# Value projection of seven head pairs: rounded and rest weights as one moving operand of 512 columns

## The chip, the cores and the metric

The kernel runs on one core of one Trainium2 chip. The metric is the device time of an execution in microseconds (us). A core has several engines that run side by side, each through a queue of its own: PE (matrix products), DVE, ACT and POOL (elementwise work), and SP, which here issues most transfers. "Row" below means one line of a view of the profile, or one instruction in an engine's order.

## The reference, cut to what matters

```python
def hybrid_mixer(h, lower_bound, w_in, ...):
    proj = h @ w_in
    xa, ga, q, f, v, g, m_a, m_b = jnp.split(proj, SPLIT_POINTS, axis=-1)
    ...
    vf = v.astype(jnp.float32).reshape(B_, S_, HG_HEADS, HG_DV)
    o = rms_norm(hgrn2_chunkwise(qf, kf, log_f, vf), hg_norm)
    ...
    return y @ w_out

def reference(x, ...):
    for l in range(DEPTH):
        h = rms_norm(x, norm_mix[l])
        x = x + hybrid_mixer(h, ...)
        h = rms_norm(x, norm_mlp[l])
        x = x + jnp.square(jax.nn.relu(h @ w_up[l])) @ w_down[l]
    return rms_norm(x, norm_final)
```

All is float32: 1024 rows of 1024 channels, 8 heads, an MLP of width 4096, one layer. The part in question is the slice v of `h @ w_in`: 1024 rows times 1024 channels of v, the sum over 1024 channels of h.

## The kernel before

Products in float32 are made from products of a shorter type. Each operand is split into a rounded part (suffix H) and a rest (suffix L), and the helper `mm3` (L157) adds three products into one PSUM bank: rounded times rounded, rounded times rest, rest times rounded. The rounded part is a cast on ACT (L94, L120), the rest a subtraction on DVE (L98); weights that are met a second time have their rest fetched back from DRAM by SP instead.

The mixer works on two halves of the rows (c = 0, 1; 512 rows each) and four pairs of heads (p = 0 to 3; 256 channels each): eight pairs of indices, one stage each. A stage projects, on PE, pj_xa, pj_q and pj_f (two banks of 128 channels by 512 rows each, weights standing still and rows moving), the gates of the recurrence pr and pi, and the values pv. The rest of the stage is the recurrence of one pair: DVE builds q, qa, qb, kb, kc, kk and qf by chains of products (L681 for all of them), PE makes small products of them (sc at L691, L811 and L822), PE turns kk around (pk, L848), multiplies it by v (pkv, L858), DVE carries the state (sn, L867 and L869), and PE makes the outputs po (L883, L886). POOL and ACT do smaller steps. Stages overlap: while PE projects for one pair, DVE works on the pair before.

The values are projected the other way round from the rest: 128 rows of h stand still (tile hT, parts H and L, 8 blocks k of 128 channels), and 256 columns of weights move. `v_steps` does this for seven of the eight pairs, for four row tiles tt of 128 rows, with 8 steps k of three matmuls each; one PSUM bank of 512 columns is taken for each row tile, and its first 256 columns are filled. ACT copies them to the tile v (L548). The pair (0,0) is projected in `first_norm` by other code. The callback `between` runs after a row tile: after the first it emits the end of the recurrence of the RG-LRU, after the second the transposes poT of outputs (L559).

The weights of the mixer come in tiles of 128 x 1024, each as two tiles with the tag "w" (rounded wH, rest wL) from one pool with six slots. The pool is also used by some weights of the gates and the MLP (names wA and ws). A slot that is to be filled again waits for the last reader of the tile that was in it. PSUM has banks under three tags: four "pj", two "sc", two "hg", handed round in turn.

The order on PE is pinned in the mixer (`pin`): it is the order of the code. The order on the other engines comes from a scheduler that goes by dependencies and priorities; `tc.high_priority(400)` moves an instruction ahead of its place. Where the MLP passes from its hidden rows to the down projection the order of PE is the scheduler's too.

Of the kernel before, what the change touches and what calls it, by code (L numbers as in the profile page):

```python
# [11 lines left out]
F32R = mybir.dt.float32r  # L12
U8 = mybir.dt.uint8
AF = mybir.ActivationFunctionType
ALU = mybir.AluOpType
# [3 lines left out]
P = 128  # L19
# [26 lines left out]
def trunk(ctx: ExitStack, tc: tile.TileContext, x, wts, mlp, pv, gains, mask_f, mask_u, out):  # L46
    nc = tc.nc
    V, A, G, PE = nc.vector, nc.scalar, nc.gpsimd, nc.tensor

    const = ctx.enter_context(tc.tile_pool(name="const", bufs=1))  # L50
    wp = ctx.enter_context(tc.tile_pool(name="wp", bufs=1))
# [55 lines left out]
    def load_w(i):  # L107
        raw = raw_tile(f"raw{i}")
        nc.sync.dma_start(raw, seq[i])
        return raw  # L110

    def split_w(i, raw):
        if i < n_mix + 3:
            h, lo = (wp.tile([P, 1024], F32R, tag="w", name=f"w{q}{i}", bufs=6) for q in "HL")
        else:
            h, lo = (kept[0].tile([P, 1024], F32R, tag=f"k{q}{i - n_mix}", name=f"w{q}{i}") for q in "HL")
        at = pair_tiles[i] if i < len(pair_tiles) else None
        with tc.high_priority(400):
            if at in rests:
                A.copy(h, raw)  # L120
                nc.sync.dma_start(lo.bitcast(F32), rests[at])
                return h, lo
            split(raw, h, lo)
        if at is not None and at in pair_tiles[i + 1 :]:
            rests[at] = dram.tile([P, 1024], F32, tag=f"rest{at}", name=f"rest{at}")
            nc.sync.dma_start(rests[at], lo.bitcast(F32))
        return h, lo
# [14 lines left out]
    used = [0]  # L142

    def next_w():
        used[0] += 1
        return get_w(used[0] - 1)
# [3 lines left out]
    def pin(ins):  # L150
        if pinned[0]:
            tc.keep_in_program_order(ins)

    def mm3(o, ah, al, bh, bl, first, last, goes_on=False, chain=None):
        how = {"skip_group_check": True} if goes_on else {}
        for a, b, begins, ends in ((ah, bh, first, False), (ah, bl, False, False), (al, bh, False, last)):
            ins = PE.matmul(o, a, b, start=begins, stop=ends, **how)  # L157
            pin(ins)
            if chain is not None:
                edge = mybir.DependencyInfo(mybir.DependencyClass.NoSync, mybir.DependencyReason.DATA)  # L160
                if chain:
                    tc.add_manual_dep(ins.ins, chain[-1].ins.name, edge, reason="last products")
                chain.append(ins)
# [142 lines left out]
    def first_norm():  # L306
# [73 lines left out]
        ws, pv = {}, {}  # L380

        def w_high(i):
            ws[i] = tuple(wp.tile([P, 1024], F32R, tag="w", name=f"w{q}{i}", bufs=6) for q in "HL")
            keep(A.copy(ws[i][0], xraws[i]))

        def w_low(i):
# [6 lines left out]
        v = mt("v", "v_00", (P, 4, 256))  # L393
# [139 lines left out]

    def v_steps(c, p, got, between):
        v = mt("v", f"v_{c}{p}", (P, 4, 256))
        w = [next_w(), next_w()]
        for tt in range(4):
            pp = bank("sc" if tt == 2 else "pj", f"pv_{c}{p}_{tt}")
            for k in range(8):
                hh, hl = kt(hT[c], k)  # L540
                cut = slice(tt * P, (tt + 1) * P)
                cols = slice((k % 4) * 256, (k % 4 + 1) * 256)
                wh, wl = w[k // 4]
                mm3(pp[:, :256], hh[:, cut], hl[:, cut], wh[:, cols], wl[:, cols], k == 0, k == 7)
                if k % 2:
                    if k < 7:
                        yield
            A.copy(v[:, tt, :], pp[:, :256])  # L548
            between(tt)
            yield  # L550
        got["v"] = v
# [540 lines left out]
    def quad_steps(i, pools, raws=raw_tile, minus=False):  # L1092

        ops = ops_w[i] = {}
        s = []

        def sums(behind=None):
            ra, rb = (r.rearrange("p (a b) -> p a b", a=2) for r in raw_q[i])
            a11, a21, a12, a22 = ra[:, 0, :], ra[:, 1, :], rb[:, 0, :], rb[:, 1, :]
            s.extend(raws(f"s{i}{h}") for h in range(2))  # L1100
            sa, sb = (r.rearrange("p (a b) -> p a b", a=2) for r in s)
            ins = V.tensor_tensor(out=sa[:, 0, :], in0=a21, in1=a22, op=ALU.add)  # L1102
            if behind is not None:
                how = mybir.DependencyInfo(mybir.DependencyClass.NoSync, mybir.DependencyReason.DATA)
                tc.add_manual_dep(ins.ins, behind.ins.name, how, reason="sums")
            if minus:
                V.scalar_tensor_tensor(sa[:, 1, :], sa[:, 0, :], -1.0, a11, op0=ALU.mult, op1=ALU.subtract)
            else:
                V.tensor_tensor(out=sa[:, 1, :], in0=sa[:, 0, :], in1=a11, op=ALU.add)
            V.tensor_tensor(out=sb[:, 0, :], in0=a21, in1=a11, op=ALU.add)  # L1110
            V.tensor_tensor(out=sb[:, 1, :], in0=a12 if minus else sa[:, 1, :], in1=sa[:, 1, :] if minus else a12, op=ALU.subtract if minus else ALU.add)

        def single(behind=None):
            t = pools[0].tile([P, 2, 512], F32R, tag="w1", name=f"wA11{i}", bufs=2)
            split(raw_q[i][0][:, 0:512], t[:, 0, :], t[:, 1, :], behind)
            ops["A11"] = (t[:, 0, :], t[:, 1, :])

        def pair(src, names):
            def go(pool=None, tag=None, bufs=None, lo_behind=None):
                if pool:  # L1120
                    t = pool.tile([P, 2, 1024], F32R, tag=tag, name=f"w{names[0]}{i}", bufs=bufs)
                    h, lo = t[:, 0], t[:, 1]
                else:
                    h, lo = (pools[1].tile([P, 1024], F32R, tag="w", name=f"w{names[0]}{i}{q}", bufs=6) for q in "HL")
                split(src(), h, lo, None, lo_behind, (names[0], i))
                for j, o in enumerate(names):
                    cols = slice(j * 512, (j + 1) * 512)
                    ops[o] = (h[:, cols], lo[:, cols])

            return go  # L1130

        return {
            "sums": sums,
            "a": single,
            "b": pair(lambda: s[0], ("s1", "s2")),
            "c": pair(lambda: s[1], ("s3", "s4")),
            "d": pair(lambda: raw_q[i][1], ("A12", "A22")),
        }
# [9 lines left out]
    for o in ("t1", "n2", "T4", "T3"):  # L1148
        pool = np_ if o in ("t1", "n2") else tp
# [314 lines left out]
    for part in range(2):  # L1464
# [4 lines left out]
        for hf in range(2):  # L1469
            pp = {tt: bank("pj", f"po1{hf}{tt}") for tt in tts}  # L1470
# [16 lines left out]
            for tt in tts:  # L1487
                cols = slice(hf * 512, (hf + 1) * 512)
# [271 lines left out]
    for kb in range(n_kb):  # L1760
        last = kb + 1 == n_kb
        qs = order[2 * kb : 2 * kb + 2]
        for half in range(2):
# [33 lines left out]
            for step, (bk, wo, uo), prs in [  # L1797
# [111 lines left out]
```

## Time and profile before

| | |
|---|---|
| time, three runs | 1534.24, 1535.8 and 1536.2 us, median 1535.8 |
| time of the profiled execution | 1535.65 us |
| its span | 1533.9 us, mean granted clock of PE 0.999 |
| HBM over the span | 199 GB/s, 201.50 MB read, 103.81 MB written |
| mixer stages with the edited code | from about 116 us to 545 us |

The span runs from the first to the last instruction in the record; the time has the 1.75 us around it as well. "Busy" counts an engine's own instructions, not its waits. Rows of a timeline give the start in us from the span's start, the length in us, the engine, the line, the operation, and output<-inputs by tile names without buffer numbers; at the end, in brackets, how long the engine was idle before and what ended that. In the rows of PE the lengths of successive matmuls overlap.

### The profile page before, as it was taken

How to read it: one execution, taken by the hardware profiler on the slowest of the kernel's cores; microseconds unless marked ns; L12 is line 12 of the kernel's file. 1: busy time of each engine (PE TensorE's matmuls, PEld its weight loads, DVE VectorE, ACT ScalarE, POOL GpSimd, SP SyncE). 2: the span in 40 equal slices, each digit the busy share in tenths (PEclk: the TensorE clock that was granted, in tenths of full speed). 3: DMA queues.
4: the chain of work that ended last, by engine and by line, in shares of the span. 5: the costliest groups of instructions: out<-in, count | busy, mean ns of one | idle time of the engine just before them, and what ended most of it. 6: DMA issues, size and time to landing. Idle time of an engine off the chain costs nothing. (4 is left out here: it accounts for less than half of the span.)

```text
span 1533.9 us, 23245 instructions
## 1 busy us (share of the span) xinstructions
PE 1521.5 (99%) x9091; PEld 1275.1 (83%) x9091; DVE 1148.0 (75%) x1661; ACT 806.4 (53%) x1346; POOL 152.3 (10%) x191
## 2 busy tenths in 40 slices
PE   9999999999999999999999999999999999999998
PEld 7878988889889888888888888888888888888886
DVE  6798696485675828786856568888788998888777
ACT  6646757567567435454533447766666722111115
POOL 1021210232614600000000000000000000000000
PEclk9999999999999999999999999999999999999999
DMA  8545455465664284432328323666666766666642
GB/s 300 198 154 200 143 193 198 150 217 173 226 230 143 97 299 160 159 137 83 138 97 327 138 110 145 267 247 247 247 252 249 262 259 264 252 248 249 240 194 110
DMA packets 82255, 306.82 MB, mean 200 GB/s; under 512 B 8545, under 2 KB 21985, under 8 KB 69218
## 3 DMA queue, kind: packets, MB, share of 16 engines
q1 hardware_dynamic: 78832, 295.24, 52.2%
q10 hardware_dynamic: 3314, 10.10, 1.7%
q8 instruction: 71, 1.16, 0.3%
q14 instruction: 38, 0.31, 0.1%
HBM read 201.50 MB, written 103.81 MB: 199 GB/s over the span
## 5 line engine op out<-in xcount | busy, mean ns | idle before, releaser
L1795 DVE TENSOR_TENSOR acc<-acc,dX 128x512 f32<-128x512 f32 x128 | 85.1, 685 | 27.7 <-PE dX L157 27.0
L94 ACT CAST wA<-q 128x512 fp32r<-128x512 f32 x46 | 28.6, 622 | 119.3 <-PE dX L157 95.4
L98 DVE TENSOR_TENSOR wL<-raw,wH 128x1024 fp32r<-128x1024 f32 x46 | 56.2, 1224 | 41.1 <-ACT wH L94 40.9
L157 PE MATMUL po<-wH,y 128*128 128x512 f32 x256 | 80.6, 391 | 0.0
L94 ACT CAST wH<-raw 128x1024 fp32r<-128x1024 f32 x46 | 48.2, 1049 | 34.2 <-DMA raw<-wts_in 14.2
L1695 POOL TENSOR_TENSOR gx<-acc,gain 128x256 f32<-128x256 f32 x1 | 0.7, 743 | 605.4 <-DVE acc L1795 605.4
L157 PEld LDWEIGHTS po<-wH,y 128*128 128x128 f32 x256 | 48.1, 188 | 9.8
L1795 DVE TENSOR_TENSOR acc<-acc,dY 128x512 f32<-128x512 f32 x64 | 43.6, 687 | 14.2 <-PE dY L157 13.8
L157 PE MATMUL po<-wL,y 128*128 128x512 f32 x128 | 49.8, 389 | 0.0
L1543 ACT ACTIVATE b<-b 128x512 f32<-128x512 f32 x48 | 30.0, 626 | 28.3 <-DVE b L1542 28.1
L98 DVE TENSOR_TENSOR wA<-q,wA 128x512 fp32r<-128x512 f32 x46 | 31.5, 686 | 15.1 <-ACT wA L94 15.1
L157 PE MATMUL uX<-h2B11H,wA 128*128 128x512 f32 x128 | 42.1, 390 | 0.0
L120 ACT CAST wH<-raw 128x1024 fp32r<-128x1024 f32 x36 | 37.8, 1049 | 8.2 <-issue 3.7
L192 POOL TENSOR_TENSOR rstd_h<-rstd_h,mhalf 128x1 f32<-128x1 f32 x8 | 4.6, 585 | 371.2 <-DVE rstd_h L187 371.2
L586 DVE SCALAR_TENSOR_TENSOR xc<-xp,pvt,xc 128x512 f32<-128x512 f32 x48 | 40.0, 844 | 1.1 <-ACT xc L570 1.1
L157 PE MATMUL gX<-hT00H,wA 128*128 128x512 f32 x112 | 36.9, 390 | 0.0
L1102 DVE TENSOR_TENSOR s<-q,q 128x512 f32<-128x512 f32 x46 | 31.6, 687 | 5.1 <-DMA q<-mlp_in 4.8
L499 POOL TENSOR_TENSOR stt<-r,stt 128x256 fp32r<-128x256 f32 x16 | 19.8, 1261 | 126.3 <-ACT stt L498 114.2
L1110 DVE TENSOR_TENSOR s<-q 128x512 f32<-128x512 f32 x46 | 31.6, 686 | 0.2
L1544 ACT ACTIVATE b<-b 128x512 f32<-128x512 f32 x48 | 30.3, 631 | 1.0
L890 ACT ACTIVATE on<-po 128x128 f32<-128x128 f32 x64 | 16.9, 278 | 26.1 <-PE po L886 26.0
L157 PEld LDWEIGHTS uX<-h2B11H,wA 128*128 128x128 f32 x128 | 24.0, 188 | 5.0
(2327 smaller groups left out, 5298.8 us busy)
## 6 DMA issues: line engine op xcount, KB each, us to landing
q<-mlp_in SPq DMA_DIRECT2D x92, 512.0 KB, 3.8
raw<-wts_in SPq DMA_DIRECT2D x80, 512.0 KB, 4.7
rest<-wL SPq DMA_DIRECT2D x36, 512.0 KB, 2.9
wL<-rest SPq DMA_DIRECT2D x36, 512.0 KB, 4.0
hd<-ri SPq DMA_DIRECT2D x16, 256.0 KB, 3.7
od<-onT ACTq DMA_DIRECT2D x8, 512.0 KB, 6.5
cdT<-stT SPq DMA_DIRECT2D x16, 256.0 KB, 3.4
o<-od SPq DMA_DIRECT2D x4, 1024.0 KB, 7.8
```

The costliest lines, as they stand in the source:

```text
L94: ins = casts[name] = A.copy(h, src)
L98: ins = V.tensor_tensor(out=lo, in0=src, in1=h.bitcast(F32), op=ALU.subtract)
L120: A.copy(h, raw)
L157: ins = PE.matmul(o, a, b, start=begins, stop=ends, **how)
L499: G.tensor_tensor(out=lo, in0=src, in1=h.bitcast(F32), op=ALU.subtract)
L586: ins = V.scalar_tensor_tensor(xc[:, s, :], xp[:, j : j + T], pvt[:, PV_CW + 8 * j + u : PV_CW + 8 * j + u + 1], xc[:, s, :], op0=ALU.mult ...
L890: A.activation(on[:, 4 * s + n, :], po[s][:, n * P : (n + 1) * P], AF.Square, accum_out=ssq[:, 4 * s + n : 4 * s + n + 1],)
L1102: ins = V.tensor_tensor(out=sa[:, 0, :], in0=a21, in1=a22, op=ALU.add)
L1110: V.tensor_tensor(out=sb[:, 0, :], in0=a21, in1=a11, op=ALU.add)
L1543: A.activation(b[:, at, :], b[:, at, :], AF.Relu, scale=-1.0 if at == 2 else 1.0)
L1544: A.activation(b[:, at, :], b[:, at, :], AF.Square)
L1795: return V.tensor_tensor(out=dst, in0=dst, in1=banks[bk, pr], op=op)
```

## The change

In `v_steps` the three matmuls of a step become two. The first has hT's rounded part standing and 512 moving columns: 256 of the rounded weights and 256 of the rest, which now lie in one tile [P, 2, 1024], so that the operand is two pieces of 256 columns, 1024 elements apart. It writes the whole bank: rounded times rounded in the first half, rounded times rest in the second. The second matmul has hT's rest standing and the 256 columns of the rounded weights moving, and adds to the first half. So v is the sum of the halves: ACT copies the second half to v, and DVE adds the first half to it, as an instruction with high priority. The number of columns that move is the same, 768 a step.

All tiles with the tag "w" become such pairs, with three slots in place of six: the mixer's weights in `split_w`, those of `first_norm`, and those of the gates and the MLP that use this pool.

```diff
+    def w_pair(pool, name):
+        t = pool.tile([P, 2, 1024], F32R, tag="w", name=name, bufs=3)
+        both_parts[name] = t
+        return t[:, 0, :], t[:, 1, :]
...
-            h, lo = (wp.tile([P, 1024], F32R, tag="w", name=f"w{q}{i}", bufs=6) for q in "HL")
+            h, lo = w_pair(wp, f"w{i}")
...
     def v_steps(c, p, got, between):
         v = mt("v", f"v_{c}{p}", (P, 4, 256))
-        w = [next_w(), next_w()]
+        w = [(both_parts[f"w{used[0]}"], next_w())[0] for _ in range(2)]
         for tt in range(4):
             pp = bank("sc" if tt == 2 else "pj", f"pv_{c}{p}_{tt}")
             for k in range(8):
                 hh, hl = kt(hT[c], k)
                 cut = slice(tt * P, (tt + 1) * P)
                 cols = slice((k % 4) * 256, (k % 4 + 1) * 256)
-                wh, wl = w[k // 4]
-                mm3(pp[:, :256], hh[:, cut], hl[:, cut], wh[:, cols], wl[:, cols], k == 0, k == 7)
+                both = w[k // 4][:, :, cols]
+                pin(PE.matmul(pp.rearrange("p (a b) -> p a b", a=2), hh[:, cut], both, start=k == 0, stop=False))
+                pin(PE.matmul(pp[:, :256], hl[:, cut], both[:, 0, :], start=False, stop=k == 7))
...
-            A.copy(v[:, tt, :], pp[:, :256])
+            A.copy(v[:, tt, :], pp[:, 256:])
+            with tc.high_priority(400):
+                V.tensor_tensor(out=v[:, tt, :], in0=pp[:, :256], in1=v[:, tt, :], op=ALU.add)
...
-                    h, lo = (pools[1].tile([P, 1024], F32R, tag="w", name=f"w{names[0]}{i}{q}", bufs=6) for q in "HL")
+                    h, lo = w_pair(pools[1], f"w{names[0]}{i}")
```

On PE, at the first row tile of the first of the seven projections (pair (0,1); pv_0 is its bank, hT00 the first four blocks of the rows), there stands before:

```order
L157 MATMUL pi_1252<-xcH_1137,wL_1043 128x512
L157 MATMUL pv_0_1335<-wH_1074,hT00H 128x256
L157 MATMUL pv_0_1335<-wL_1075,hT00H 128x256
L157 MATMUL pv_0_1335<-wH_1074,hT00L 128x256
L157 MATMUL pv_0_1335<-wH_1074,hT00H 128x256
L157 MATMUL pv_0_1335<-wL_1075,hT00H 128x256
L157 MATMUL pv_0_1335<-wH_1074,hT00L 128x256
```

and of the change:

```order
L164 MATMUL pi_1234<-xcH_1120,w_1027 128x512
L551 MATMUL pv_0_1315<-w_1058,hT00H 128x512
L552 MATMUL pv_0_1315<-w_1058,hT00L 128x256
L551 MATMUL pv_0_1315<-w_1058,hT00H 128x512
L552 MATMUL pv_0_1315<-w_1058,hT00L 128x256
```

Two steps are shown, six rows before and four now; what stands around the projection on PE is the same as before. (Line numbers after the change are 7 to 10 higher.)

On DVE, in the stage that works on pair (1,1), between the gate f and the products for qb, there stands before:

```order
L674 TENSOR_SCALAR f_4091<-f_4091 128x1024
L681 TENSOR_TENSOR q_3852<-q_3852,f_4091 128x512
...
L681 TENSOR_TENSOR qa_4103<-qa_4103,seg_4102 128x128x2x2
L681 TENSOR_TENSOR seg_4102<-seg_4102 128x128 x3
L681 TENSOR_TENSOR qb_4109<-qa_4103,seg_4102 128x32x4x2
L681 TENSOR_TENSOR kc_4117<-kb_4105,seg_4102 128x128x6
L681 TENSOR_TENSOR qb_4109<-qa_4103,seg_4102 128x32x4x2 x2
L681 TENSOR_TENSOR seg_4102<-seg_4102 128x128
```

and of the change:

```order
L684 TENSOR_SCALAR f_3925<-f_3925 128x1024
L558 TENSOR_TENSOR v_3961<-pv_0_3972,v_3961 128x256
L691 TENSOR_TENSOR q_3689<-q_3689,f_3925 128x512
...
L691 TENSOR_TENSOR qa_3937<-qa_3937,seg_3936 128x128x2x2
L558 TENSOR_TENSOR v_3961<-pv_1_3998,v_3961 128x256
L691 TENSOR_TENSOR seg_3936<-seg_3936 128x128 x3
L691 TENSOR_TENSOR qb_3943<-qa_3937,seg_3936 128x32x4x2
L558 TENSOR_TENSOR v_3961<-pv_2_4031,v_3961 128x256
L691 TENSOR_TENSOR kc_3951<-kb_3939,seg_3936 128x128x6
L691 TENSOR_TENSOR qb_3943<-qa_3937,seg_3936 128x32x4x2 x2
L558 TENSOR_TENSOR v_3961<-pv_3_4050,v_3961 128x256
L691 TENSOR_TENSOR seg_3936<-seg_3936 128x128
```

The four adds of the stage stand one by one among the products for qa, qb and kc; the order of these is the same. Later in this stage the first step of the convolution (L586) stands ahead of the copy into dd at L710 instead of behind it.

On DVE, in the first stage, where the carried state sn is made from pkv of two heads, there stands before:

```order
L98 TENSOR_TENSOR xcL_1138<-xc_811,xcH_1137 128x1024
L673 TENSOR_SCALAR f_1166<-f_1166,par 128x512
L98 TENSOR_TENSOR wL_1197<-raw_1194,wH_1196 128x1024
L673 TENSOR_SCALAR f_1166<-f_1166,par 128x512
L867 COPY sn_1185<-pkv_1175 128x128
L674 TENSOR_SCALAR f_1166<-f_1166 128x1024
L869 SCALAR_TENSOR_TENSOR sn_1185<-sn_1185,seg_720,pkv_1175 128x128
```

and of the change:

```order
L98 TENSOR_TENSOR xcL_1121<-xc_798,xcH_1120 128x1024
L683 TENSOR_SCALAR f_1149<-f_1149,par 128x512
L877 COPY sn_1168<-pkv_1158 128x128
L879 SCALAR_TENSOR_TENSOR sn_1168<-sn_1168,seg_709,pkv_1158 128x128
L98 TENSOR_TENSOR w_1179<-raw_1177,w_1179 128x1024
L683 TENSOR_SCALAR f_1149<-f_1149,par 128x512
L879 SCALAR_TENSOR_TENSOR sn_1168<-sn_1168,seg_709,pkv_1158 128x128
L684 TENSOR_SCALAR f_1149<-f_1149 128x1024
```

The state of the first head is begun ahead of the rest of a weight tile and of the second f, that of the second head later than before. A little ahead of this place, in the same stage, two copies into xp (L584) that stood ahead of kc and qb now stand behind qf, and one product q (L660) stands ahead of kc instead of behind it.

More of the change, by code (lines that the diff above doesn't have):

```diff
@@ L110, in load_w @@
         return raw
+    both_parts = {}
+    def w_pair(pool, name):
+        t = pool.tile([P, 2, 1024], F32R, tag="w", name=name, bufs=3)
+        both_parts[name] = t
+        return t[:, 0, :], t[:, 1, :]
     def split_w(i, raw):
         if i < n_mix + 3:
-            h, lo = (wp.tile([P, 1024], F32R, tag="w", name=f"w{q}{i}", bufs=6) for q in "HL")
+            h, lo = w_pair(wp, f"w{i}")
         else:
@@ L382, in w_high @@
         def w_high(i):
-            ws[i] = tuple(wp.tile([P, 1024], F32R, tag="w", name=f"w{q}{i}", bufs=6) for q in "HL")
+            ws[i] = w_pair(wp, f"w{i}")
             keep(A.copy(ws[i][0], xraws[i]))
```

## The prediction, made before the change was run

> **What bounds the kernel now.** I read the page first, its engines and slices:
>
> ```profile
> span 1533.9 us, 23245 instructions
> PE 1521.5 (99%) x9091; PEld 1275.1 (83%) x9091; DVE 1148.0 (75%) x1661; ACT 806.4 (53%) x1346; POOL 152.3 (10%) x191
> PE   9999999999999999999999999999999999999998
> PEclk9999999999999999999999999999999999999999
> ```
>
> PE is busy for 1521.5 of 1533.9 us, in every slice, at the full granted clock (0.999 in the record of this run). So the end moves by what PE issues less, or by what it is made to wait. The view of the waits, kept to PE, lists what it waits for today; its columns are us in total, times, longest:
>
> ```profile
> PE gain L331 <- POOL gain_row L321: 2.5, 1, 2.5
> PE po L883 <- DVE sn L869: 0.9, 1, 0.9
> PE dX L157 <- DMA u8n<-u8n: 0.7, 1, 0.7
> PE sc L822 <- DVE qf L681: 0.5, 1, 0.5
> ```
>
> The first lies in the start, before the changed lines; the second and fourth in the first mixer stage; the third in the MLP. None lies in the seven stages that the change edits, up to 0.2 us pieces that the view lists below these. The same by stretches of the span (busy time and instructions of PE, PEld, DVE, ACT and POOL):
>
> ```profile
> 30.00:115.00 85.00, 83.30 (x614) 68.59 (x614) 69.27 (x140) 50.38 (x88) 10.11 (x13) 1.00 0.55 194
> 180.00:240.00 60.00, 60.00 (x562) 52.02 (x561) 46.89 (x83) 37.72 (x75) 5.89 (x11) 1.00 0.45 159
> 363.00:425.00 62.00, 62.00 (x567) 53.62 (x566) 40.52 (x68) 41.65 (x85) 24.84 (x29) 1.00 0.61 209
> ```
>
> From 180 on PE has no idle time at all, while DVE is free for 13 of 60 and 21 of 62 us. What is left is the pace of PE itself. The timeline of PE around one value projection (start, length, then the instruction):
>
> ```profile
> 359.82 0.39 PE L157 MATMUL pj_f<-hT11H,wH 128*128 128x512 f32 x1
> ...
> 363.67 0.39 PE L157 MATMUL pj_f<-hT11H,wL 128*128 128x512 f32 x1
> 363.90 0.28 PE L157 MATMUL pv<-wH,hT10H 128*128 128x256 f32 x1
> ...
> 369.65 1.04 PE L559 MATMUL poT<-ident,on 128*128 128x128 f32 x8
> ...
> 376.15 0.28 PE L157 MATMUL pv<-wH,hT11L 128*128 128x256 f32 x1
> 376.27 0.40 PE L157 MATMUL pj_xa<-hT10H,wH 128*128 128x512 f32 x1
> ```
>
> Lengths overlap, so the price of a matmul is the step from one start to the next. Between 359.82 and 363.90 stand 18 matmuls of 512 columns: 4.08 / 18 = **226.7 ns**. Between 363.90 and 369.65 stand 48 of 256 columns (two row tiles of 8 steps of 3): 5.75 / 48 = **119.8 ns**. Twice the columns cost 106.9 ns more, 0.418 ns a column, so each matmul, with the weight load that goes with it, carries 119.8 - 106.9 = 12.9 ns that no column pays for. The two changes of width are priced alike: 512 then 256 takes 0.23 (363.67 to 363.90), 256 then 512 takes 0.12 (376.15 to 376.27).
>
> The Trainium skill, in "TensorE: Matmul & The Clock Gate", section "Wait — 56ns, not 53.3ns?", puts the fixed cost of a warm matmul at about 2.5 ns on top of its columns at 2.4 GHz, which speaks against this change. By it the sum below would be 224 x 2.5 = 0.56 us, an estimate from that page. The trace's slope agrees with 2.4 GHz, its 12.9 ns does not agree with 2.5.
>
> **The change part by part.**
>
> *The matmuls.* Seven pairs, 4 row tiles, 8 steps: 224 steps. A step was three matmuls of 256 columns, 3 x 119.8 = 359.4 ns; it becomes one of 512 and one of 256, 226.7 + 119.8 = 346.5. That is 12.9 ns a step and 224 x 12.9 = **2.9 us** in all, 0.41 in each of the seven stages. Not shown in the trace is a moving operand in two pieces of 256 columns that lie a tile apart. Its nearest rows are the 512 columns in one piece, 226.7, and two matmuls of 256, 239.6; a saving below zero would need it to be dearer than two instructions, for which no row gives a reason. I take the first, since width and type are the same; ends 2.9 and 0. Below the 119.8 of the remaining matmul lie only its columns, 106.9: if its load hid under the wider matmul before it, another 224 x 12.9 = 2.9 would go. The step of 0.23 and 0.12 at the changes of width says that it does not.
>
> *The copies on ACT* stay 28 of the same size; they only read the other half of the bank:
>
> ```profile
> L548 ACT COPY v<-pv x28: 355/380/427, 124.2 to 502.1; 128x256 f32<-128x256 f32 x28
> ```
>
> *The adds on DVE* are new: 28 of 128x256, one operand in PSUM. These are DVE's and PE's rows of the stage of pair (1,1):
>
> ```profile
> 372.58 0.87 DVE L681 TENSOR_TENSOR q<-q,f 128x512 f32<-128x512 f32 x1
> ...
> 383.75 0.69 DVE L681 TENSOR_TENSOR qb<-qb,seg 128x512 f32<-128x512 f32 x1
> ...
> 386.55 0.42 DVE L681 TENSOR_TENSOR dd<-sc,mf 128x256 f32<-128x256 f32 x1
> ...
> 389.27 0.45 DVE L710 COPY_PREDICATED dd<-mu,sc 128x192 f32<-128x192 uint8 x1 [1.82 <-PE sc L691]
> 389.99 0.75 DVE L586 SCALAR_TENSOR_TENSOR xc<-xp,pvt,xc 128x512 f32<-128x512 f32 x1 [0.27 <-ACT xc L570]
> ...
> 403.74 1.37 DVE L98 TENSOR_TENSOR xcL<-xc,xcH 128x1024 fp32r<-128x1024 f32 x1 [0.64 <-ACT xcH L94]
> 405.65 0.75 DVE L660 SCALAR_TENSOR_TENSOR q<-sq,par,pj_q 128x512 f32<-128x512 f32 x1 [0.54 <-ACT sq L658]
> 407.09 0.75 DVE L660 SCALAR_TENSOR_TENSOR q<-sq,par,pj_q 128x512 f32<-128x512 f32 x1 [0.69 <-ACT sq L658]
> 407.75 0.68 DVE L681 TENSOR_TENSOR kk<-kk,seg 128x512 f32<-128x512 f32 x1
> ```
>
> ```profile
> 392.07 0.33 PE L691 MATMUL sc<-qb,kc 128*32 128x48 f32 x11
> 408.55 0.71 PE L848 MATMUL pk<-ident,kk 128*128 128x128 f32 x5
> ```
>
> The dd row has the same shape and a PSUM operand, so an add costs 0.42, four of them 1.68 a stage, 11.8 us of DVE in all. They are placed between 372.58 and 384 (second fence of the change). Behind them on DVE stand the rest of qa, qb and kc, and PE asks for qb at 392.07, 7.6 after the qb row ends (384.44). Then DVE comes to a wait for PE of 1.82 (389.27); after that it waits for ACT four times, 0.27 + 0.64 + 0.54 + 0.69 = 2.14. The adds need 1.68, and PE is 0.41 earlier: 2.09 of 3.96. The last two waits matter most: q, which stands ahead of kk, hangs on products of PE itself, so kk keeps its distance to pk. That is small: kk ends at 408.43, pk starts at 408.55. I cost the adds at **0**; without cover it is 1.68 - 0.12 = 1.56 us a stage. v itself is first read behind pk, some 30 us on. The four banks of the projections go round in turn, so the first row tile's goes to the second half of pj_xa, from 376.5; its add stands right ahead of q (372.58) and is done by then.
>
> Does an add wait? It needs its row tile's last matmul and ACT's copy:
>
> ```profile
> 371.59 0.40 ACT L548 COPY v<-pv 128x256 f32<-128x256 f32 x1
> ...
> 375.54 1.05 ACT L120 CAST wH<-raw 128x1024 fp32r<-128x1024 f32 x1
> ...
> 376.82 0.37 ACT L548 COPY v<-pv 128x256 f32<-128x256 f32 x1
> ...
> 379.71 0.37 ACT L548 COPY v<-pv 128x256 f32<-128x256 f32 x1
> ```
>
> The first copy ends at 371.99, before DVE comes to q at 372.58; the last at 380.08, when the fourth add cannot start before 381. ACT now takes a cast of a weight tile (1.05, as at 375.54) ahead of the second copy, which puts its end at 378.2, about where DVE comes to it. Nothing to half a microsecond of DVE, inside the 1.87 of cover that is left.
>
> *The pair tiles.* Three slots of rounded and rest together replace six single ones, so the cast of a slot waits for the readers of both halves. The rest was read by the middle matmul of a step, the rounded part by the last, so the slot comes free at the same matmul: **0**, ends 0 and one step, 0.35.
>
> *What else moves.* In the first stage DVE takes the state of the first head of the pair earlier (third fence of the change), for which PE waits 0.9 now, and the copies into xp stand behind qf, for which it waits 0.5. Both could shrink by up to these, together 1.4; against it stands one q product ahead of kc there, 0.75. I take **0.3** gained, ends 1.4 gained and 0.75 lost. In the MLP some casts, adds to acc and two loads change places between the hidden rows and the down projection, where the order is not pinned. PE's largest wait in that half is 0.7, so I take **0**, ends 0.7 either way.
>
> *Sum.* 1535.65 - 2.9 - 0.3 = **1532.4 us** on the profiled execution, which lies 0.15 under the median of the three runs, 1535.8, so nothing is corrected for it.
>
> **The rivals.**
>
> *No gain.* The operand in two pieces costs what two matmuls cost, or the 12.9 ns belong to each piece that is read. Then 2.9 is gone and 1535.65 - 0.3 = **1535.3** is left. For it: no row shows such an operand. Against it: the same width in one piece. If only part of the 12.9 ns goes with the number of matmuls, a fifth say, 224 x 2.6 = 0.6 is saved: 1535.65 - 0.6 - 0.3 = 1534.8. That belongs here too, with 0.04 of this rival's 0.21, since the prices of both widths and of their changes fit one fixed cost. The Trainium skill's 2.5 ns would have it about so.
>
> *Slower: the adds reach the path.* The place is kk to pk, margin 0.12, here in the stage before too:
>
> ```profile
> 346.59 0.69 DVE L681 TENSOR_TENSOR kk<-kk,seg 128x512 f32<-128x512 f32 x1
> 347.38 0.39 PE L848 MATMUL pk<-ident,kk 128*128 128x128 f32 x2
> ```
>
> If the adds, the waits for their copies and the moved steps of the convolution together outgrow the 3.96 of cover, every further microsecond on DVE is one on PE. Priced with nothing covered, in the four stages from 302 to 545: 1535.65 - 2.9 + 4 x 1.56 = **1539.0**. For it: margins of a tenth, adds with high priority ahead of work that PE asks for. Against it: 2.09 of 3.96, and q's tie to PE. It decides from about 1.9 us a stage on top of the adds, and passes the time of before only from 2.9 / 4 = 0.7 us lost a stage.
>
> *More gain.* The waits of the first stage go (1.4), or the loads of the 256-column matmuls hide (2.9 more): 1535.65 - 2.9 - 1.4 = **1531.3**, down to 1528.4 with both.
>
> **How the numbers follow.** Forecast 0.56, no gain 0.21, more gain 0.12, slower 0.11. A difference of 0.2%, 3.07 us, is about what a measurement of this kernel tells from none; from 1535.8 that is 1532.7, close above the forecast. With ends of some half microsecond on the small terms I put 0.35 of the forecast's 0.56 below it: faster 0.35 + 0.12 = 0.47; same 0.21 + 0.21 and 0.01 of the slower rival = 0.43; slower 0.10. The range runs from 1530.0, which leaves out the second half of "more gain" (0.06), to 1536.2, which takes in "no gain" with the 0.75 lost in the first stage and leaves out the slower rival (0.10).
>
> **What would show it.** In the changed kernel pv rows should alternate steps of 0.227 and 0.120 and the two blocks of a projection take 32 x 0.1733 = 5.54 instead of 5.75. A step of 0.24 for the wide one is "no gain"; 0.107 for the narrow one is "more gain". The wait of 1.82 at dd should shrink to nearly nothing and no wait of PE at pk for kk may appear; one of 1.5 in each stage is the slower rival. The 28 adds should read 0.42. The prediction is wrong in its small terms if PE's list of waits shows a new one of over half a microsecond in the first stage or at the start of the down projection.

## The result, and the profile after

The changed kernel takes **1544.18 us** (median of 5 runs, 1543.52 to 1545.41) beside 1535.2 (5 runs, 1534.24 to 1536.2) for the kernel before: ratio 1.0059, 95% interval 1.0048 to 1.007. It is slower by 0.6%, outside the range predicted and on the other side of the forecast. Its profiled execution took 1544.34 us, 8.69 more than that of before.

The page of the changed kernel, span, engines and the slices of PE:

```profile
span 1542.6 us, 22748 instructions
PE 1522.7 (99%) x8867; PEld 1264.2 (82%) x8867; DVE 1153.9 (75%) x1689; ACT 803.9 (52%) x1346; POOL 157.0 (10%) x191
PE   9999999999999899999999999999999999999998
```

PE has 224 matmuls fewer and is busy 1.2 us *longer*; one slice, the fourteenth (501 to 540 us), is no longer full. The list of PE's waits (us in total, times, longest):

```profile
PE sc L701 <- DVE qb L691: 4.3, 1, 4.3
PE gain L338 <- POOL gain_row L328: 2.5, 1, 2.5
PE pkv L868 <- ACT kT L863: 1.0, 2, 0.6
PE poT L569 <- ACT on L915: 0.8, 2, 0.4
PE xT_x L371 <- DVE xn L362: 0.7, 1, 0.7
PE dX L164 <- DMA u0n<-u0n: 0.7, 1, 0.7
PE po L893 <- DVE rstd_x L194: 0.6, 1, 0.6
PE po L893 <- DVE sn L879: 0.5, 1, 0.5
```

One wait alone is 4.3 us, and before there was none at that place. Below these the list has three of 0.3 us in the MLP that the kernel before does not show (at xT_h, dZ and uX). The PE rows of that instruction in the kernel before and in the changed one:

```profile
514.42 0.89 PE L691 MATMUL sc<-qb,kc 128*32 128x48 f32 x64
```

```profile
520.55 1.07 PE L701 MATMUL sc<-qb,kc 128*32 128x48 f32 x64 [4.33 <-DVE qb L691]
```

The wait has a second price. The changed kernel by stretches (length, PE busy and instructions, granted clock, DMA share, GB/s):

```profile
516.00:520.50 4.50, 0.22 (x1) 1.00 0.04 17
520.50:522.00 1.50, 1.45 (x65) 0.70 0.32 123
522.00:524.00 2.00, 2.00 (x6) 0.50 0.40 146
524.00:526.00 2.00, 2.00 (x10) 0.87 1.09 383
526.00:528.00 2.00, 2.00 (x10) 1.00 0.39 135
```

After 4.33 us without work PE gets half the clock for some 3 us, and 6 matmuls start in 2 us where 10 do at full clock. That is why PE's busy time grew. (A stretch that mixes both clocks shows their mean, as 0.70 and 0.87 here.)

Laying the starts of the same PE instructions in both traces side by side gives the whole account (us; each row is one instruction, the last is the span):

| PE instruction | before | after | later by | of it new |
|---|---|---|---|---|
| pr, first stage | 113.05 | 114.47 | +1.4 | +1.4 |
| pv behind the first poT | 125.31 | 127.76 | +2.5 | +1.0 |
| third pkv | 224.15 | 227.22 | +3.1 | +0.6 |
| poT of the fifth projection | 369.65 | 372.15 | +2.5 | -0.6 |
| poT of the last projection | 492.01 | 493.91 | +1.9 | -0.6 |
| sc of the last mixer stage | 514.42 | 520.55 | +6.1 | +4.2 |
| mb, behind it | 523.53 | 531.20 | +7.7 | +1.5 |
| end of the span | 1533.9 | 1542.6 | +8.7 | +1.0 |

So the saving is there, 0.29 to 0.31 us at each projection, and everything around it costs more. Each kernel stands here with one profiled execution. Of the first 1.4, some 0.4 is there already at the first pj_xa (25.50 before, 25.89 after), a place that lies between 25.5 and 25.8 us in the traces with single tiles and between 25.4 and 26.1 in those with pairs; the first stage itself makes 1.0.

**Why qb is late in the last mixer stage.** POOL there has a burst of work (r, stt, stT: sums of blocks of hT), which `last_stage` emits behind the last value projection. POOL's first rows of it before and after:

```profile
502.81 7.88 POOL L499 TENSOR_TENSOR stt<-r,stt 128x256 fp32r<-128x256 f32 x2 [20.29 <-ACT stt L498]
```

```profile
504.99 2.48 POOL L506 TENSOR_TENSOR stt<-r,stt 128x256 fp32r<-128x256 f32 x2 [20.25 <-ACT stt L505]
```

The same two subtractions take 7.88 us before and 2.48 after; POOL alone does one in 0.74. DVE's rows say the reverse. Before:

```profile
504.81 0.68 DVE L1102 TENSOR_TENSOR s<-q,q 128x512 f32<-128x512 f32 x1
505.42 0.41 DVE L681 TENSOR_TENSOR qb<-qa,seg 128x256 f32<-128x256 f32 x1
...
508.40 1.75 DVE L644 TENSOR_TENSOR_SCAN ri<-a,hcar,ri 128x512 f32<-128x512 f32 x1
510.08 1.16 DVE L681 TENSOR_TENSOR qb<-qb,seg 128x512 f32<-128x512 f32 x1
```

and after:

```profile
506.07 0.42 DVE L558 TENSOR_TENSOR v<-pv,v 128x256 f32<-128x256 f32 x1
506.80 1.23 DVE L1112 TENSOR_TENSOR s<-q,q 128x512 f32<-128x512 f32 x1 [0.30 <-DMA q<-mlp_in]
...
510.74 0.97 DVE L691 TENSOR_TENSOR qb<-qa,seg 128x256 f32<-128x256 f32 x1
...
519.35 1.14 DVE L691 TENSOR_TENSOR qb<-qb,seg 128x512 f32<-128x512 f32 x1
```

The reader is to see the two regimes. Before, POOL started at 502.81 and its first subtraction ended only at 509.07, behind the start of DVE's scan at 508.40; DVE ran at full pace (s 0.68, qb 0.41), and qb was done at 511.24, 3.2 us ahead of PE. After, POOL came in at about the fourth add (506.07), and from there the two engines took turns: each DVE row is some 0.55 us longer (s 1.23, qb 0.97). Twelve instructions and a scan stand between that add and the end of qb. Eleven of the twelve are 0.5 to 0.6 longer than the same rows before, 6.0 together; the scan is 0.5 shorter, since before it was the scan that met POOL. qb ended at 520.49, 9.25 us later than before: 2.2 for the later start of the chain (its f starts at 496.43 and started at 494.20), 4 x 0.34 = 1.4 for the adds from start to start, 0.3 for the pause for a load, and some 5.4 for the turns.

The Trainium skill, "SBUF — State Buffer", section "Who interferes with whom", says that DVE and GpSimd (POOL here) share a pair of ports, that a DVE instruction with two inputs in SBUF contends with a GpSimd instruction that reads SBUF, and that one with at most one input in SBUF does not, outside the modes with two ports. The traces agree so far: the products have two inputs in SBUF, and the add reads PSUM. Why POOL gets in at the scan, whose inputs a and ri lie in SBUF too, no run shows.

### The profile page after: what moved, and what is told of

Read it like the earlier page. It is cut to its first block, busy times and chain, and to the rows that moved or that the text cites. A ratio compares the mean times of both kernels' runs of the same rounds, so it can differ in the third digit from the quotient of the medians.

```text
span 1542.6 us, 22748 instructions
## 1 busy us (share of the span) xinstructions
PE 1522.7 (99%) x8867; PEld 1264.2 (82%) x8867; DVE 1153.9 (75%) x1689; ACT 803.9 (52%) x1346; POOL 157.0 (10%) x191
## 5 line engine op out<-in xcount | busy, mean ns | idle before, releaser
L94 ACT CAST ws<-s 128x1024 fp32r<-128x1024 f32 x92 | 96.4, 1050 | 130.8 <-PE dY L164 52.8
L94 ACT CAST wA<-q 128x512 fp32r<-128x512 f32 (+1 forms) x92 | 76.6, 835 | 126.9 <-PE dX L164 104.5
L98 DVE TENSOR_TENSOR ws<-s,ws 128x1024 fp32r<-128x1024 f32 x92 | 112.2, 1222 | 31.6 <-ACT ws L94 31.6
L98 DVE TENSOR_TENSOR wA<-q,wA 128x512 fp32r<-128x512 f32 (+1 forms) x92 | 87.2, 954 | 44.9 <-ACT wA L94 44.8
L98 DVE TENSOR_TENSOR w<-raw,w 128x1024 fp32r<-128x1024 f32 x41 | 50.1, 1223 | 33.3 <-ACT w L94 32.3
L94 ACT CAST w<-raw 128x1024 fp32r<-128x1024 f32 x41 | 42.9, 1048 | 20.8 <-issue 13.4
L127 ACT CAST w<-raw 128x1024 fp32r<-128x1024 f32 x36 | 37.6, 1045 | 22.9 <-PE pj_f L164 7.7
L164 PE MATMUL uX<-h2T4H,wA 128*128 128x512 f32 x128 | 42.4, 392 | 0.4 <-DVE b L1552 0.3
L164 PE MATMUL uZ<-h2B21H,wA 128*128 128x512 f32 x128 | 42.1, 390 | 0.0
L164 PE MATMUL uX<-h2n2H,ws 128*128 128x512 f32 x128 | 42.0, 389 | 0.0
L164 PE MATMUL uY<-h2B22H,ws 128*128 128x512 f32 x128 | 42.0, 389 | 0.0
```

The lines of the kernel that those rows point to most:

```text
L94: ins = casts[name] = A.copy(h, src)
L98: ins = V.tensor_tensor(out=lo, in0=src, in1=h.bitcast(F32), op=ALU.subtract)
```

## The experiments

All were run beside the kernel before, at 1535.17 to 1535.33 us. The first four split the change into its parts.

**The pair tiles alone** (`e1_pairs`): the changed kernel with the old three matmuls and the old copy, without adds.

```diff
-                pin(PE.matmul(pp.rearrange("p (a b) -> p a b", a=2), hh[:, cut], both, start=k == 0, stop=False))
-                pin(PE.matmul(pp[:, :256], hl[:, cut], both[:, 0, :], start=False, stop=k == 7))
+                mm3(pp[:, :256], hh[:, cut], hl[:, cut], both[:, 0, :], both[:, 1, :], k == 0, k == 7)
```

> The pair tiles alone: weights in pair tiles with three slots, but the old three matmuls of 256 columns and no adds. Theory A (the loss is made in the last mixer stage, where POOL takes turns with DVE and each DVE instruction of the chain to qb is 0.55 us longer): DVE's order there is that of before, so PE waits less than 0.3 us for qb and the time is 1535 to 1537, with the small waits of the first stages and the down projection (up to 2 us in the changed kernel) if the pair tiles make those. Theory B (the adds' own time on DVE): same here, 1535 to 1536. Theory C (the pair tiles reorder the weights' casts and rests, and that makes the loss): 1541 or more.

Measured: 1537.82 us, ratio 1.0019 [1.001, 1.0028]. No wait for qb, but the first stage has these waits of the changed kernel:

```profile
PE pkv L865 <- ACT kT L860: 0.6, 1, 0.6
PE po L890 <- DVE rstd_x L194: 0.6, 1, 0.6
```

The tiles alone, which the prediction had at 0, cost 2.5 us by the medians. The profiled execution is 2.0 us longer than that of before: pr of the first stage starts 1.3 later, the third pkv 1.5, and behind mb another 0.4 comes. 0.3 of it stands ahead of the first stage, so that 1.0 is the first stage's, as in the changed kernel: from the products sc at 96.44 us to pr pass 16.61 us before and 17.60 here.

**The split sum and the adds alone** (`e2_adds`): the kernel before, with the two halves of the bank and the adds, from single tiles and three matmuls.

```diff
-                mm3(pp[:, :256], hh[:, cut], hl[:, cut], wh[:, cols], wl[:, cols], k == 0, k == 7)
+                pin(PE.matmul(pp[:, :256], hh[:, cut], wh[:, cols], ...))
+                pin(PE.matmul(pp[:, 256:], hh[:, cut], wl[:, cols], ...))
+                pin(PE.matmul(pp[:, :256], hl[:, cut], wh[:, cols], ...))
...
-            A.copy(v[:, tt, :], pp[:, :256])
+            A.copy(v[:, tt, :], pp[:, 256:])
+            with tc.high_priority(400):
+                V.tensor_tensor(out=v[:, tt, :], in0=pp[:, :256], in1=v[:, tt, :], op=ALU.add)
```

> The adds alone: tiles as before, three matmuls of 256 columns, of which the middle one writes the second half of the bank; the same copies and 28 adds as in the change. No saving on PE. Theory A: four adds displace the chain and a sum that waits for its load stands ahead of the rest of qb as in the changed kernel, so POOL gets its turn early: a wait for qb of 2 to 5 us, time 1538 to 1543. Theory B: 4 x 0.42 = 1.7 us against a distance of 3.2 us, no wait, 1535 to 1536. Theory C: 1535 to 1536.

Measured: 1541.49 us, ratio 1.0039 [1.0024, 1.0054]. The wait is there without pair tiles and without a wide matmul:

```profile
PE sc L695 <- DVE qb L685: 2.8, 1, 2.8
```

So is the lower clock around its end: from 518.3 to 521.6 us the granted clock is 0.50. The parts do not add up to the whole: 6.2 us for the adds, 2.5 for the tiles and 2.1 saved by the matmuls give 6.6, and the change costs 9.0; with all of them together the wait for qb is 4.3 instead of 2.8.

**The last projection in the old way** (`e5_last_old`): the changed kernel, where pair (1,3) alone has three matmuls, the old copy and no add (`c + p == 4` picks it out).

> The changed kernel, but the last of the seven projections, pair (1,3), made the old way: three matmuls of 256 columns, one copy, no adds. Theory A (the loss is made where four adds displace the chain to qb in the last mixer stage and POOL takes turns with it): DVE's order there is that of before, no wait for qb, no fall of the clock: 1544.2 - 4.3 - 1.5 + 0.3 for the saving of that stage = 1538.7, give or take 0.7. Theory B (the adds cost about the same in every stage): one seventh of the loss goes, 1543.

Measured: 1537.83 us, ratio 1.0015 [1.0006, 1.0025]: 6.35 us less than the changed kernel, for four adds and one projection of seven. No wait for qb, and POOL is kept out again:

```profile
504.91 7.95 POOL L506 TENSOR_TENSOR stt<-r,stt 128x256 fp32r<-128x256 f32 x2 [20.22 <-ACT stt L505]
```

**The wide matmul only in the four middle projections** (`e9_quiet`), where PE waits for nothing; the others as in `e5_last_old`.

> The changed kernel with the wide matmul and its adds only in the four projections whose stages showed no new wait, (0,3), (1,0), (1,1) and (1,2); the other three the old way; all weights in pair tiles. Theory A with the places read so far: the pair tiles alone cost 2.5 us (first stages and start of the down projection), four projections save 0.29 each, nothing else: 1535.3 + 2.5 - 1.2 = 1536.6, give or take 0.6. If the adds cost something wherever they stand, it is not below the pair tiles alone, 1537.8.

Measured: 1536.78 us, ratio 1.0012 [1.0003, 1.0021]. It is the best of the change's family and still not faster than the kernel before: what four projections save (1.2) does not pay for the pair tiles (2.5). The median is 1.0 us below that of the pair tiles alone, near the saving that was expected, but the two intervals overlap.

A version with the pair tiles as parts of one tile (`e8_ring`, 1552.83 us) was to take their cost away. It does not compute the same values, its order on the engines is another one as well, and its time tells nothing on the slots:

> As the kernel with four wide projections, but the three pairs of weight tiles are parts of one tile that is used in turn, so that a cast or a rest waits for the readers of its own part alone. If the 2.5 us of the pair tiles come from the slots being freed together, they go, and the time is 1535.3 - 1.2 = 1534.1, which would beat both kernels; if they come from the order that the scheduler happens to find, this one has another order again, and anything from 1534 to 1541 is possible.

The next ones ask why the last stage is dear. **POOL's burst moved away from the chain** (`e3_pool`): the changed kernel, with the burst behind the first half of g.

```diff
         yield from v_of(NC * NPAIR)
-        combos_on(2)
...
             if c == 0:
-                combos_on(1)
+                combos_on(3)
```

> The changed kernel with the two steps of POOL's combination work that are emitted at the start of the last mixer stage moved behind the first half of its first projection. Theory A: DVE's chain to qb runs at its unstretched length, PE waits less than 0.5 us for qb, its clock stays up, and the time is 1544.2 - 4.3 - 1.4 = 1538.5, give or take 0.7. Theory B and C: the wait stays, 1543.5 to 1544.5.

Measured: 1539.77 us, ratio 1.0026 [1.0016, 1.0037], 0.6 above the interval expected. The wait for qb is gone and the clock stays full, so the adds' own length does not make the wait. Instead PE waits 1.5 us at pk for kk, a later chain, which the burst now meets.

**The burst moved ahead** (`e6_pool_early`): the kernel before, with `combos_on(2)` ahead of the last value projection.

> The kernel before, without any part of the change; the two steps of POOL's combination work of the last mixer stage are emitted ahead of the value projection there instead of behind it, so POOL can start about 3 us earlier. Theory A: POOL alone is enough: if it gets its turns before DVE has passed qb, some 10 to 16 instructions are 0.55 us longer and PE waits 2 to 5 us for qb, 1537.5 to 1541. If DVE's run of instructions with two operands in SBUF keeps POOL out until the first scan, as in the kernel before, POOL's first subtraction takes some 9 us and the time stays at 1535 to 1536. Theory B: 1535 to 1536, with nothing longer on DVE.

Measured: 1539.0 us, ratio 1.0029 [1.0019, 1.0038]. The profiled execution, 1541.32 us, is one of the longer ones; in it PE waits 3.9 us for qb. The number came near, the reason did not: DVE stood still for a load that the burst's new place delayed.

```profile
511.36 1.05 DVE L1102 TENSOR_TENSOR s<-q,q 128x512 f32<-128x512 f32 x1 [5.89 <-DMA q<-mlp_in]
```

On the regimes this run shows one thing more. POOL's first subtraction was kept out for 5.80 us, until DVE stopped at 505.48; it ended at 506.07. While DVE stood still POOL took 0.72 to 0.74 an instruction, and when DVE went on, with no add among its rows, its next four rows took turns with POOL (1.05, 0.96, 1.23 and 0.96) until POOL had nothing left to do. So a long enough pause of DVE lets POOL in as well.

**The pause for the load taken away** (`e4_hold`): the changed kernel, with the MLP's sums s held behind qb by a dependency (`gwork[q]["sums"](gots[-1]["qb"])`).

> The changed kernel with one dependency more: the sums of MLP weights on DVE in the last mixer stage, which had waited 0.30 us for a load, stand behind the last product for qb. POOL's work stays where it is. Theory A in its sharper form (POOL is kept out as long as DVE runs without a pause, and that pause of 0.30 let it in): POOL's first subtraction takes 5 us or more, DVE's instructions up to the first scan keep their length, the wait for qb is under 1 us and the time 1538 to 1539.5. If POOL takes its turns without a pause of DVE, 12 instructions less two sums still are 0.55 us longer: the wait falls only to about 2, time 1541 to 1542.5. Theory B and C: 1542.5 to 1544.

Measured: 1542.68 us, ratio 1.0039 [1.0025, 1.0053]. The five runs lie in two groups, 1539.8 and 1540.0 and three from 1542.7 to 1543.0; the profile is one of the upper group. In it there is no pause any more, yet POOL's first subtraction is as short as in the changed kernel (1.78 us in both), and the wait is still there, 1.8 us:

```profile
505.00 2.64 POOL L506 TENSOR_TENSOR stt<-r,stt 128x256 fp32r<-128x256 f32 x2 [20.24 <-ACT stt L505]
```

So the theory that it took the pause of 0.3 us to let POOL in fell. The shorter wait is that of a chain with two instructions fewer in it.

**The adds at ordinary priority** (`e7_noprio`: the line with `tc.high_priority(400)` left out).

> The changed kernel with the adds at ordinary priority: in the last mixer stage three of the four stand behind the chain to qb and the two scans. Theory A: the chain passes before POOL's burst as in the kernel before, no wait for qb and no fall of the clock, 1544.2 - 5.8 = 1538.4; the banks of the projection come free later, which may cost PE up to 2 us where the next projection asks for them, and the small waits at pkv and poT of the first stages (1.5 us) may go: 1537 to 1540.5. Theory B: the adds take the same time, 1543.5 to 1544.5.

Measured: 1544.49 us, ratio 1.0052 [1.0036, 1.0069]. That is above the interval of theory A, and the number is the one of theory B, for another reason. The last qb ends at 515.37, POOL is kept out up to the scan again, and other waits take the place of that for qb, since PE now waits for a bank that a late add still holds, 2.3 us up to 209.3 and 3.6 in the last mixer stage:

```profile
PE sc L700 <- DVE v L557: 6.0, 2, 3.6
```

What was left in common was the add itself: it reads PSUM. **One such instruction put into the kernel before** (`e10_door`) and **the same with both inputs in SBUF** (`e11_door_sbuf`, `in0=v[:, tt, 32:64]`); nothing reads its result.

```diff
             A.copy(v[:, tt, :], pp[:, :256])
+            if c + p == 4 and tt == 3:
+                with tc.high_priority(300):
+                    V.tensor_tensor(out=mt("vs", "vs", (P, 32)), in0=pp[:, :32], in1=v[:, tt, :32], op=ALU.add)
```

> The kernel before, with one instruction more on DVE in the last mixer stage, right behind kc: 128x32, one input in PSUM, its result not used. In the kernel before, POOL's first subtraction of the burst (502.8) is kept out for 6.3 us by DVE and gets in only at the scan (508.4). Theory D (a DVE instruction with two inputs in SBUF holds POOL out, and one that reads PSUM lets it in): POOL's first subtraction ends right behind the new instruction, after 2 to 3 us instead of 6.3, from there DVE's rows up to the last qb are 0.5 us longer each (some 8 of them, about 4.1 us more than in the kernel before), qb ends past PE's need (3.2 us of distance), and PE waits 0.5 to 1.5 us at sc for qb: 1536.3 +- 0.6. Rival L (only the length of what is added on DVE counts, or POOL gets in by chance): 0.1 us more on DVE, first subtraction 6.3 as before, no wait for qb, 1535.3 +- 0.4.

> The control of the run before: the same instruction at the same place on DVE, same size, but both inputs in SBUF. Theory D: POOL's first subtraction is kept out 6 us or more up to the scan, no wait of PE for qb, 1535.3 +- 0.4. Rival (any further instruction there shifts POOL's entry): the same as its sister, first subtraction 2 to 3 us and a wait at sc for qb.

Measured: 1536.64 us, ratio 1.0009 [1.0, 1.0018], with PSUM, and 1535.65, ratio 1.0002 [0.9993, 1.0012], with SBUF. The intervals overlap, but the medians differ by 1.0 us, and seven of the eleven runs with SBUF are below all eleven with PSUM. The traces show where it comes from. With PSUM, the list of waits, then POOL and DVE:

```profile
PE sc L694 <- DVE qb L684: 0.7, 1, 0.7
```

```profile
503.34 3.82 POOL L499 TENSOR_TENSOR stt<-r,stt 128x256 fp32r<-128x256 f32 x2 [20.30 <-ACT stt L498]
```

```profile
505.34 0.18 DVE L551 TENSOR_TENSOR vs<-pv,v 128x32 f32<-128x32 f32 x1
505.44 1.13 DVE L1105 TENSOR_TENSOR s<-q,q 128x512 f32<-128x512 f32 x1
506.49 0.95 DVE L684 TENSOR_TENSOR qb<-qa,seg 128x256 f32<-128x256 f32 x1
...
514.42 1.16 DVE L684 TENSOR_TENSOR qb<-qb,seg 128x512 f32<-128x512 f32 x1
```

and with SBUF:

```profile
503.28 6.95 POOL L499 TENSOR_TENSOR stt<-r,stt 128x256 fp32r<-128x256 f32 x2 [20.31 <-ACT stt L498]
```

```profile
505.27 0.76 DVE L551 TENSOR_TENSOR vs<-v 128x32 f32<-128x32 f32 x1
505.95 0.68 DVE L1105 TENSOR_TENSOR s<-q,q 128x512 f32<-128x512 f32 x1
506.56 0.41 DVE L684 TENSOR_TENSOR qb<-qa,seg 128x256 f32<-128x256 f32 x1
```

Behind an instruction of 0.18 us that reads PSUM the regime in which DVE keeps POOL out is over: the next seven rows of the chain are longer by about half a microsecond each, and qb ends at 515.58. Behind its twin it is not: s and qb keep 0.68 and 0.41, and the last qb ends at 512.39 (511.24 in the kernel before, whose stage starts half a microsecond earlier). One part of the expectation for the twin fell. Its own row is 0.76 long, and the first of POOL's two subtractions got in there, after 2.70 us; only the second was kept out, for 4.3 us, up to the scan. So a narrow instruction with two inputs in SBUF can let one POOL instruction pass as well.

**The adds with both inputs in SBUF** (`e12_sbuf_hold`): as `e4_hold`, and in the last projection ACT copies the whole bank.

```diff
+            if c + p == 4:
+                vs = mt("vs", f"vs_{tt}", (P, 512), bufs=2)
+                A.copy(vs, pp)
+                with tc.high_priority(400):
+                    V.tensor_tensor(out=v[:, tt, :], in0=vs[:, :256], in1=vs[:, 256:], op=ALU.add)
```

> The changed kernel with the MLP's sums held behind qb, as in e4_hold, and in the last mixer stage ACT copies both halves of the bank (512 columns instead of 256), so that the four adds have both inputs in SBUF. Theory D: the adds no longer let POOL in, its first subtraction is kept out for 5 us or more, the wait for qb (1.8 to 2.0 in e4_hold) is gone, and the time comes near e5_last_old: 1537.8 +- 0.8. Rival L (the adds' length on DVE and the burst behind it make the wait, whatever they read): wait 1.5 to 2, 1542.7 +- 1.0.

Measured: 1538.8 us, ratio 1.0024 [1.0014, 1.0034], 0.2 above the interval expected. The median is 3.9 us below that of `e4_hold`, but the intervals overlap, since `e4_hold` has two runs near 1540; here too the traces say more. The wait for qb is gone, and POOL is out until the scan; its row:

```profile
504.65 7.25 POOL L506 TENSOR_TENSOR stt<-r,stt 128x256 fp32r<-128x256 f32 x2 [20.93 <-ACT stt L505]
```

In the same part PE still waits 0.8 us at pk for kk. One more thing differs between the two: ACT copies twice the columns here, and the last add stands behind kc instead of ahead of two rows of seg.

None of the versions is faster than the kernel before.

## Why the prediction was wrong

*The matmuls* (2.9 predicted): the mechanism was right, the size was 2.1. PE's rows of a projection after:

```profile
366.50 0.39 PE L551 MATMUL pv<-w,hT10H 128*128 128x512 f32 x1
366.73 0.28 PE L552 MATMUL pv<-w,hT10L 128*128 128x256 f32 x1
366.84 0.40 PE L551 MATMUL pv<-w,hT10H 128*128 128x512 f32 x1
...
372.15 1.04 PE L569 MATMUL poT<-ident,on 128*128 128x128 f32 x8
```

From 366.50 to 372.15 stand 16 steps: 5.65 / 16 = 353 ns a step, beside 359.4 before and 346.5 predicted. Here the wide matmul took 236 ns on the mean (227 to 241), not 226.7, and the narrow one 117: the operand in two pieces is dearer than one piece and a little cheaper than two matmuls. The second block of a projection took 5.64 instead of 5.83, so a projection saves 0.29 to 0.31 us, and seven 2.1. "No gain" was wrong as well.

*The copies on ACT* did stay as they were (28, 0.38 us each), and *the adds* measured 0.42 as read from dd:

```profile
L558 DVE TENSOR_TENSOR v<-pv,v 128x256 f32<-128x256 f32 x28 | 11.8, 420 | 0.0
```

*"I cost the adds at 0"* is the step that failed. Its cover, 3.96 us, was read in the stage of pair (1,1) and taken for all seven. In the middle stages it held: from 308 to 492 PE gained at each projection and waited for nothing, and in the stage of pair (1,1) DVE's waits of 1.82 and 2.14 us are used up. The last mixer stage is another one. DVE has MLP work there beside the chain, POOL has its burst, and the distance from qb to PE is 3.2 us instead of 7.6. There the four adds added 1.4 us and, above all, POOL came in behind one of them. The price was 4.2 us of wait and 1.5 of lowered clock, 5.7 of the 8.7; `e5_last_old` gives 6.35 back. In an early stage the adds cost too: from the second pkv to the third pass 63.18 us before, 63.36 in `e1_pairs` and 64.17 in `e2_adds`, where PE waits 0.8 at the third for ACT's kT. How ACT comes to be late there was not tried apart. The two waits for poT are not the adds', which stand later on DVE. There ACT waits 2.1 us for a POOL instruction (hrs, 128x8) that takes 8.25 us in the changed kernel, 3.53 before, 1.74 in `e1_pairs` and 3.52 in `e12_sbuf_hold` (1.65 in the later stages), although the order on DVE up to there is the same in the three kernels with pair tiles. So the order on DVE alone does not settle when POOL gets in.

*The pair tiles* (0, at most 0.35) cost 2.5 by `e1_pairs`. The argument, that a slot comes free at the same matmul, speaks of the value projection only; of the time, 1.0 went in the first stage, and the traces place the rest less surely. *What else moves* had the first stage wrong: it lost 1.0 (17.6 instead of 16.6 us from sc to pr, in every trace with pair tiles but that of `e8_ring`) instead of gaining 0.3. One half of the argument came true, PE's wait for the first head's state shrank from 0.93 to 0.51. But the second head's state, which the change moves back, ends later and PE waits for it. Its last sn rows on DVE and the PE row behind them, before and after (the view names rstd_x, which follows sn on DVE):

```profile
110.73 0.34 DVE L869 SCALAR_TENSOR_TENSOR sn<-sn,seg,pkv 128x128 f32<-128x128 f32 x1
111.57 0.61 PE L883 MATMUL po<-v,scT 128*128 128x128 f32 x4
```

```profile
112.08 0.75 DVE L879 SCALAR_TENSOR_TENSOR sn<-sn,seg,pkv 128x128 f32<-128x128 f32 x2
112.89 0.71 PE L893 MATMUL po<-v,scT 128*128 128x128 f32 x4 [0.60 <-DVE rstd_x L194]
```

From one group of po to the other pass 2.40 us instead of 1.64, 0.8 lost; another 0.5 goes ahead of pkv, where ACT's kT comes later. Behind mb the changed kernel lost 1.0 instead of 0, about the sum of its three new waits of 0.3; that is one execution of each, and which moved instruction makes them is open.

*The rival "slower: the adds reach the path"* had the right sign and the right part of the change, with a wrong place and price: not kk to pk by 1.56 us in four stages, but qb to sc once, by turns with POOL. It priced an instruction on DVE by its own length only. The row that could have warned was in the trace of before: POOL's two subtractions of 7.88 us, where others of that size take 0.74.

The Trainium skill's page "TensorE: Matmul & The Clock Gate", section "What's actually happening", gives half the clock after an idle window of about 3.4 us. The 4.33 us of idle time here agree (0.50); `e2_adds` fell to 0.50 as well after 2.8 us, which is shorter than that, and `e4_hold` kept 1.00 after 1.8.

## What to carry to other kernels

Read the cover for a new instruction in every stage where it will stand, and above all in the one that differs from the others; the smallest distance decides, not the typical one. Where DVE and POOL work at the same time, look at how long POOL's rows are beside the same rows elsewhere: a POOL row of several times its usual length may be one that DVE keeps out, and what you insert may end that, at half a microsecond for each DVE instruction that follows. A saving of a tenth of a per cent on a full engine is paid back by one wait of a few microseconds, and by the clock that falls behind it.

## What the runs showed of the hardware that was not expected

- Two regimes between DVE and POOL: shut out (one POOL subtraction took 6.3 us instead of 0.74, DVE at full pace) or by turns (both go on, each DVE row 0.55 us longer). In the three traces where a DVE add that reads PSUM, even one of 0.18 us, runs while POOL is kept out, POOL's subtraction ends 0.7 us after the add's start (the changed kernel, `e4_hold`, `e10_door`); with the adds from SBUF it stayed out (`e12_sbuf_hold`). PSUM is not the only way in: POOL also got in at a scan, in a pause of DVE (`e6_pool_early`), in `e2_adds` at once, at 504.39, during products of seg that follow an add by 0.4 us, in `e11_door_sbuf` once through a narrow instruction, and in the first stage after 1.7 to 8.3 us with the same order on DVE. Each of these traces is one execution, so how large a part chance has is not shown, and what decides between turns and shutting out after an entry stays open.
- A wait has an echo: 4.33 us of idle PE took the granted clock to 0.50 and cost 1.5 us more; 2.8 us took it to 0.50 as well, and 1.8 us left it full.
- A moving operand of two pieces of 256 columns: 236 ns on the mean, beside 226.7 for 512 in one piece and 239.6 for two matmuls; the 256-column matmul behind it stepped in 117 instead of 119.8.
